# Another order of the projections in the second block of a two-block hybrid network (one NeuronCore, float32)

## The chip, the cores and the metric

The kernel runs on one core of one Trainium2 chip. The metric is the device time of one execution in microseconds (us); the time before is a median of three runs. Engine names are those of the profile: PE is TensorE (matmul), PEld its weight load, DVE is VectorE, ACT is ScalarE, POOL is GpSimd, SP is SyncE, which issues the loads of the weights.

## The reference, cut to what matters

Two blocks run one after the other on 512 positions of width 1024. The change lies in the mixer of the second. It projects the normalised input with one matrix into 14 groups of columns, lets three branches work on them, and projects the joined result with `w_out`:

```
p = xn @ w_in                       # (512, 1024) @ (1024, 3340)
mq, mk, mv, mo, mi, mf, lx, lg, aq, ak, av, iq, ik, iw = split_cols(p)
hA = mlstm_chunkwise(mq, mk, mv, mi + b_igate, mf + b_fgate)   # 4 heads of 96: matrix memory
hA = rmsnorm(hA, mlstm_norm) * sigmoid(mo)
xc = causal_depthwise_conv(lx, lru_conv_w, lru_conv_b)
hB = rglru(xc, ...) * gelu(lg)                                 # linear recurrence, 384 channels
hC = dsa_attention(aq, ak, av, iq, ik, iw)                     # 4 heads of 64, 128 chosen keys a query
mix = concatenate([hA, hB, hC]) @ w_out
x = x + rmsnorm(mix); x = x + rmsnorm(conv_ffn(rmsnorm(x)))
```

`dsa_attention` scores every admissible key for a query with `iq`, `ik` and `iw`, keeps the best 128, and runs a softmax attention with `aq`, `ak`, `av` over those alone.

## The kernel before

**Tiling.** Activations lie with the channel on the partition: eight tiles of 128 channels by 512 positions. A weight tile (128x1024, 512 KB) is loaded as `raw` by SP, rounded by ACT into `wh`, and DVE takes the remainder `wl = raw - wh`. Each step of a projection is three matmuls (activation by `wh`, activation by `wl`, remainder of the activation by `wh`). A unit of kind `f` (128 output channels by 512 positions) is 8 such steps, 24 matmuls of 512 columns. A unit of kind `tok` has the positions on the partition and 256 channels as columns; it takes two weight tiles, and is 96 matmuls of 256 columns, 24 for each of the four blocks of positions t.

**What sets the order.** Every engine works through its own list in order. The lists are written when the kernel is built, by a planner (`Model`, `Lane`, `Build`) that keeps an estimated time of each engine. `block2_mix` (L1434) walks down the table `UNITS2` (L1355): the first four entries are computed together, the others one after the other. After each step, `tick` (L200) lets every side task whose inputs are due by the estimate emit its next instructions, so that their matmuls stand between those of the projections. The engines then wait for real at whatever is not ready, and everything behind the waiting instruction on that engine's list waits too. Rounds of the top-k search are handed to DVE one by one, when it has nothing else.

**The side tasks of the mixer**, with what each waits for:
- `scores` (L1505) starts once `iq1` is done: for t = 1, 2, 3 the index scores on PE, ReLU on ACT, weighting on DVE; then 16 rounds of top-k on DVE (MAX8 and MATCH_REPLACE8 over 256, 384 or 512 columns) and the mask `mbs` of that t.
- `sparse` (L1720), sixteen steps (t, head) in three streams, needs `aq`, `ak`, `av` and the mask of its t. `sparse_out` (L1774) turns the result into `hc[6]` and `hc[7]`.
- `lrus` (L1547) needs `lx0` to `lx2`, in its last part `lg0` to `lg2`, and makes `hc[3]` to `hc[5]`.
- `memory` (L1604), four heads in two streams, needs the gates, `mk`, `mq`, and `va`, which is done with unit `t1`. Its last matmuls (128x97) are copied into two tiles `nums` (names `act<-at`, 128x194).
- `memories` (L1660), behind the last of them: maximum of the denominators (`den`), squares on ACT (128x768, twice), sums of them on DVE (`sumsq`, twice), a chain of 17 small DVE instructions ending in `rd`, and then, once unit `t2` is done and its gate `mo` went through Tanh, per half a multiplication by `rd` (128x768) and two by the gate; 12 transposes on PE, an ACT copy and a DVE subtraction for each of three tiles give `hc[0]` to `hc[2]`.

After the table, `w_out` is multiplied (`units` with `order=[3, 4, 5, 0, 1, 2, 6, 7]`, 24 matmuls of 256 columns for an output tile and half of the positions). When it comes to a tile of `hc` that is not there by the plan, it takes another that is; the first output tiles of the first half are begun with what is there.

Of the kernel before, what the change touches and what calls it, by code (L numbers as in the profile page):

```python
# [162 lines left out]
class Build:  # L163
# [1075 lines left out]
    def block1_ffn(self):  # L1239
# [114 lines left out]

    UNITS2 = [  # L1355
        ('idx',),
        ('aq0', 'f', 2312),
        ('lg0', 'f', 1928),
        ('aq1', 'f', 2440),
        ('lx0', 'f', 1544),  # L1360
        ('lx1', 'f', 1672),
        ('lx2', 'f', 1800),
        ('iq0', 'f', 3080),
        ('mk0', 'f', 384),
        ('lg1', 'f', 2056),
        ('lg2', 'f', 2184),
        ('iq1', 'f', 3208),
        ('mk1', 'f', 512),
        ('av', 'tok', 2824),
        ('mk2', 'f', 640),  # L1370
        ('mq0', 'f', 0),
        ('mq1', 'f', 128),
        ('t0', 'tok', 768),
        ('mq2', 'f', 256),
        ('t1', 'tok', 1024),
        ('ak0', 'f', 2568),
        ('ak1', 'f', 2696),
        ('t2', 'tok', 1280),
    ]

# [826 lines left out]
```

## Time and profile before

| | us |
|---|---|
| median of 3 runs (lowest, highest) | 1567.85 (1567.51, 1568.6) |
| the profiled execution: its time, its span | 1567.5, 1565.7 |
| PE busy | 1546.3 (99%) |
| DVE busy | 1101.5 (70%) |
| ACT busy | 680.5 (43%) |
| weight load (PEld) busy, beside the matmuls | 1386.4 (89%) |
| granted TensorE clock, mean | 0.999 |

The mixer of the second block takes the stretch from about 936 us to 1190 us. The rows are given below; in a timeline row the first number is the start in us from the start of the span, the second the time to the end of the last instruction of the row, and a bracket at the end is the idle time ahead of it with what ended it. Matmuls are pipelined: one that is listed with 0.28 us follows the one ahead after 0.12 us.

### The profile page before, as it was taken

What the parts mean: (1) busy time and instruction counts of PE and PEld (TensorE: products, weight loads), DVE (VectorE), ACT (ScalarE), POOL (GpSimd) and SP (SyncE); (2) the same over time, 40 slices, a digit from 0 to 9 for tenths busy, and PEclk for the clock granted to TensorE, in tenths of its full rate; (3) what the DMA queues carried; (4) which work ended last, traced back from release to release, by engine and by line L of the source; (5) the groups of instructions that cost most, each with busy time, mean ns of one, the idle gap of its engine ahead of it and who ended that gap; (6) DMA issues with size and microseconds to landing.
All of it is one profiled execution on the core that took longest, in us unless ns stands there. A gap on an engine that the chain in (4) does not pass through costs nothing.

```text
span 1565.7 us, 25299 instructions
## 1 busy us (share of the span) xinstructions
PE 1546.3 (99%) x10279; PEld 1386.4 (89%) x10281; DVE 1101.5 (70%) x2011; ACT 680.5 (43%) x1222; POOL 25.9 (2%) x89
## 2 busy tenths in 40 slices
PE   7999999999999999999999999999999999999998
PEld 6999999999999999999988877796799888888886
DVE  4899999997764576776743457899768877775224
ACT  5344544546843343443432223625565544444112
POOL 4000000000000000000000000000000000000000
PEclk9999999999999999999999999999999999999999
DMA  5322222222222333333333332231053133333221
GB/s 145 95 69 75 75 70 80 68 68 68 73 77 71 92 108 93 85 94 95 91 88 98 84 99 80 59 104 55 19 144 109 55 95 95 95 98 102 94 95 68
DMA packets 233005, 134.17 MB, mean 86 GB/s; under 512 B 6925, under 2 KB 228240, under 8 KB 232888
## 3 DMA queue, kind: packets, MB, share of 16 engines
q1 hardware_dynamic: 231448, 130.35, 28.7%
q8 instruction: 81, 1.33, 0.4%
q0 software_dynamic: 1136, 1.15, 0.3%
q10 hardware_dynamic: 304, 1.05, 0.2%
q14 instruction: 36, 0.29, 0.1%
HBM read 130.44 MB, written 2.10 MB: 85 GB/s over the span
## 4 chain that ended last, share of the span: by engine, by line
PE 97%; DVE 1%; ACT 1%; DMA 0%; issue 0%; DVEq 0%; ACTq 0%; POOLq 0%
PE mm L314 70%; PE at L314 24%; PE at L320 3%; ACT act L158 1%; DVE act L158 0%; DMA act<-in_x_dram 0%; DVE yy L158 0%; DVE wl L158 0%; ACT ys L158 0%; DVE yc L158 0%; ACT wh L158 0%; DVE nb L158 0%; DVE fx L158 0%; DVE res L158 0%; ACT e L158 0%
## 5 line engine op out<-in xcount | busy, mean ns | idle before, releaser
L314 PE MATMUL mm<-act,wh 128*128 128x256 f32 (+3 forms) x4720 | 906.2, 306 | 1.5 <-DVE act L158 0.8
L314 PEld LDWEIGHTS mm<-act,wh 128*128 128x128 f32 (+1 forms) x4720 | 692.0, 189 | 49.5 <-issue 10.9
L314 PE MATMUL mm<-act,wl 128*128 128x256 f32 (+4 forms) x2360 | 562.8, 302 | 0.0
L158 ACT ACTIVATE wh<-raw 128x1024 fp32r<-128x1024 f32 (+2 forms) x235 | 245.7, 1047 | 367.5 <-PE mm L314 187.1
L158 DVE TENSOR_TENSOR wl<-raw,wh 128x1024 fp32r<-128x1024 f32 (+2 forms) x235 | 284.5, 1211 | 168.9 <-ACT wh L158 165.9
L314 PEld LDWEIGHTS mm<-act,wl 128*128 128x128 f32 (+1 forms) x2360 | 383.1, 189 | 18.0
L158 DVE SCALAR_TENSOR_TENSOR act<-u,par,act 128x514 f32<-128x514 f32 x232 | 161.1, 748 | 2.2 <-ACT act L158 2.2
L314 PE MATMUL at<-act,wh 128*128 128x512 f32 x416 | 130.3, 394 | 0.0
L314 PEld LDWEIGHTS at<-act,wh 128*128 128x128 f32 x416 | 78.1, 188 | 18.4
L314 PE MATMUL at<-wh,act 128*128 128x512 f32 x264 | 86.0, 395 | 0.0
L314 PE MATMUL mm<-wh,act 128*128 128x256 f32 (+1 forms) x344 | 84.4, 320 | 0.0
L314 PE MATMUL at<-act,act 128*128 128x256 f32 (+9 forms) x468 | 83.5, 329 | 0.8 <-ACT act L158 0.7
L314 PE MATMUL at<-act,wl 128*128 128x512 f32 x208 | 82.0, 394 | 0.0
L158 DVE TENSOR_TENSOR act<-act,act 128x514 f32<-128x514 f32 (+4 forms) x122 | 69.7, 589 | 8.2 <-ACT act L158 7.5
L314 PEld LDWEIGHTS at<-act,act 128*128 128x128 f32 (+1 forms) x468 | 60.2, 189 | 11.1 <-issue 4.7
L158 DVE SCALAR_TENSOR_TENSOR ft<-fx,par,ft 128x512 f32<-128x512 f32 x88 | 65.8, 749 | 1.5
L158 DVE TENSOR_TENSOR fx<-mm,rB 128x514 f32<-128x514 f32 x44 | 30.5, 694 | 50.3 <-PE mm L314 50.1
L314 PEld LDWEIGHTS mm<-wh,act 128*128 128x128 f32 x344 | 57.9, 189 | 7.3 <-issue 3.4
L158 ACT ACTIVATE act<-mm 128x528 f32<-128x528 f32 (+2 forms) x64 | 35.1, 548 | 66.8 <-PE mm L314 66.7
L158 ACT ACTIVATE act<-at 128x128 f32<-128x128 f32 (+6 forms) x88 | 34.4, 413 | 67.8 <-PE at L314 50.2
L158 DVE SCALAR_TENSOR_TENSOR gy<-gx,par,gy 128x512 f32<-128x512 f32 x84 | 62.6, 748 | 1.5
L314 PEld LDWEIGHTS at<-wh,act 128*128 128x128 f32 x264 | 49.6, 188 | 11.6
(286 smaller groups left out, 1435.8 us busy)
## 6 DMA issues: line engine op xcount, KB each, us to landing
raw<-in_w_in_dram SPq DMA_DIRECT2D x82, 512.0 KB, 3.8
raw<-in_w_up_dram SPq DMA_DIRECT2D x44, 512.0 KB, 3.8
raw<-in_ffn_up_dram SPq DMA_DIRECT2D x44, 512.0 KB, 3.9
raw<-in_ffn_down_dram SPq DMA_DIRECT2D x22, 512.0 KB, 3.2
raw<-in_w_out_dram SPq DMA_DIRECT2D x20, 512.0 KB, 3.8
raw<-in_w_down_dram SPq DMA_DIRECT2D x16, 512.0 KB, 3.8
raw<-in_w_conv_out_dram SPq DMA_DIRECT2D x8, 512.0 KB, 3.8
raw<-in_w_down_dram SPq DMA_DIRECT2D x8, 384.0 KB, 3.3
```

The source lines that it names most:

```text
L158: return f(*a, **k)
L314: self.nc.tensor.matmul(out, lhsT, rhs, start=start, stop=stop)
L320: self.nc.tensor.transpose(out, src, self.ident[p0 : p0 + k, p0 : p0 + k])
```

## The change

The entries of `UNITS2` get another order; nothing else is edited. Entries and their number stay the same, and so do the instructions of each engine; what the planner puts between the projections follows the new order.

```
     UNITS2 = [
         ('idx',),
+        ('iq0', 'f', 3080),
+        ('iq1', 'f', 3208),
         ('aq0', 'f', 2312),
-        ('lg0', 'f', 1928),
-        ('aq1', 'f', 2440),
         ('lx0', 'f', 1544),
         ('lx1', 'f', 1672),
         ('lx2', 'f', 1800),
-        ('iq0', 'f', 3080),
+        ('lg0', 'f', 1928),
         ('mk0', 'f', 384),
+        ('aq1', 'f', 2440),
+        ('mk1', 'f', 512),
         ('lg1', 'f', 2056),
+        ('mk2', 'f', 640),
         ('lg2', 'f', 2184),
-        ('iq1', 'f', 3208),
-        ('mk1', 'f', 512),
         ('av', 'tok', 2824),
-        ('mk2', 'f', 640),
         ('mq0', 'f', 0),
+        ('ak0', 'f', 2568),
         ('mq1', 'f', 128),
         ('t0', 'tok', 768),
+        ('ak1', 'f', 2696),
         ('mq2', 'f', 256),
         ('t1', 'tok', 1024),
-        ('ak0', 'f', 2568),
-        ('ak1', 'f', 2696),
         ('t2', 'tok', 1280),
     ]
```

On PE, the list is the same up to the start of the mixer's units and again from the second output tile of `w_out` on; some 800 entries between are rearranged. Before, this stood on PE from the last product of the memory (`128x97`) to the first transposes of its result (`ident` with a name of 128x768); `mm_11435` and `mm_11436` are unit `t2`, `mm_11889` is `w_out`, the `128x64` and those with `e` or `mbs` are the sparse attention:

```order
L314 MATMUL at_11684<-act_10935,act_11505 128x97
L314 MATMUL mm_11435<-wh_11342,act_9580 128x256
...
L320 MATMUL at_11748<-ident,e_11740 128x128 x3
...
L314 MATMUL at_11829<-act_11334,act_10107 128x384
...
L314 MATMUL mm_11436<-wh_11342,act_9857 128x256
L320 MATMUL at_11879<-ident,e_11865 128x128 x3
L314 MATMUL mm_11889<-act_10700,wh_11442 128x256 x2
...
L314 MATMUL at_11936<-act_11334,act_10107 128x512
...
L314 MATMUL at_11944<-act_10631,act_10762 128x64 x4
L320 MATMUL at_11954<-ident,act_11898 128x128 x2
```

Now the same stretch reads (`mm_11562` is unit `t2`, `mm_11953` is `w_out`, `act_12007` and `act_12011` the two halves of the memory's result):

```order
L314 MATMUL at_11917<-act_11037,act_11837 128x97
L314 MATMUL mm_11562<-wh_11565,act_9765 128x256
...
L314 MATMUL mm_11562<-wh_11565,act_9857 128x256
L314 MATMUL mm_11953<-act_10742,wh_11582 128x256 x2
...
L314 MATMUL mm_11953<-act_10816,wh_11582 128x256 x2
L314 MATMUL mm_11953<-act_10816,wl_11583 128x256
L320 MATMUL at_12015<-ident,act_12007 128x128 x2
L320 MATMUL at_12015<-ident,act_12011 128x128 x2
L320 MATMUL at_12023<-ident,act_12007 128x128 x2
L320 MATMUL at_12023<-ident,act_12011 128x128 x2
L314 MATMUL mm_11953<-act_12020,wh_11582 128x256 x2
```

What moved: between the last product and the first transposes there were 95 matmuls, 45 of `t2` and `w_out` and 50 of the sparse attention with its transposes; there are 15 now, 6 of `t2` and 9 of `w_out`. The sparse attention stands ahead of the memory's last head.

On ACT, in the same place, the list had the squares (`128x768`) ahead of the Tanh of the gates (`128x512`, `128x1024`), with copies and exponentials of the sparse attention between:

```order
L158 ACTIVATE act_11237<-at_11684 128x2x97
L158 ACTIVATE act_10762<-at_11748 128x384
...
L158 ACTIVATE act_11779<-act_11236 128x768
L158 ACTIVATE e_11789,sll_11769<-at_11756,snb_11768 128x384
L158 ACTIVATE act_11575<-mm_11435,R 128x256
L158 ACTIVATE act_11797<-act_11237 128x768
...
L158 ACTIVATE act_11575<-mm_11436,R 128x256
L158 ACTIVATE act_10477<-act_10477 128x512
L158 ACTIVATE act_11575<-act_11575 128x1024
```

Now, from the copy of the memory's last products on:

```order
L158 ACTIVATE act_11569<-at_11917 128x2x97
L158 ACTIVATE act_11653<-mm_11562,R 128x256
L158 ACTIVATE act_10694<-act_10694 128x512
L158 ACTIVATE act_11653<-act_11653 128x1024
L158 ACTIVATE wh_11960<-raw_11563 128x1024
L158 ACTIVATE act_11970<-act_11568 128x768
L158 ACTIVATE wh_11978<-raw_11580 128x1024
L158 ACTIVATE act_11983<-act_11569 128x768
```

What moved: the Tanh of the gates and two weight roundings of `w_out` now stand ahead of the squares.

On DVE, the part of `memories` from `den` to the small chain had narrow instructions of the sparse attention between its own; now it has two remainders `wl` of 128x1024:

```order
L158 SCALAR_TENSOR_TENSOR den<-act_11236 128x8
L158 TENSOR_REDUCE sumsq<-act_11779 128x8
L158 SCALAR_TENSOR_TENSOR den<-act_11237 128x8
L158 TENSOR_SCALAR act_10763<-at_11781,srl_11724 128x64
L158 TENSOR_SCALAR act_10763<-at_11785,srl_11728 128x64
L158 TENSOR_REDUCE sumsq<-act_11797 128x8
L158 TENSOR_TENSOR den<-den,em 128x16
```

Now, from the first `den` on:

```order
L158 SCALAR_TENSOR_TENSOR den<-act_11568 128x8
L158 TENSOR_TENSOR wl_11961<-raw_11563,wh_11960 128x1024
L158 TENSOR_REDUCE sumsq<-act_11970 128x8
L158 SCALAR_TENSOR_TENSOR den<-act_11569 128x8
L158 TENSOR_TENSOR wl_11979<-raw_11580,wh_11978 128x1024
L158 TENSOR_REDUCE sumsq<-act_11983 128x8
L158 TENSOR_TENSOR den<-den,em 128x16
```

What moved: the remainders wait for the roundings of ACT that stand ahead of the squares there.

## Rows read from the trace of the kernel before

**Rows 1.** The page: busy time and share of PE, and the shares of the engines in the chain of work that ended last.

```profile
PE 1546.3 (99%) x10279; PEld 1386.4 (89%) x10281; DVE 1101.5 (70%) x2011; ACT 680.5 (43%) x1222; POOL 25.9 (2%) x89
...
PE 97%; DVE 1%; ACT 1%; DMA 0%; issue 0%; DVEq 0%; ACTq 0%; POOLq 0%
```

**Rows 2.** Busy time of each engine by stretch (from and to in us, length, then us busy with the number of instructions for PE, PEld, DVE, ACT and POOL, the granted clock, the DMA share and GB/s).

```profile
1000.00:1057.00 57.00, 57.00 (x370) 49.51 (x366) 54.61 (x124) 22.20 (x46) 0.22 (x2) 1.00 0.30 84
...
1120.00:1143.00 23.00, 21.99 (x158) 18.41 (x159) 15.61 (x39) 12.99 (x26) 0.20 (x2) 1.00 0.16 47
1143.00:1190.00 47.00, 46.52 (x395) 46.51 (x395) 35.09 (x73) 33.32 (x67) 0.10 (x1) 1.00 0.47 133
```

**Rows 3.** Timeline of PE at the end of the mixer: the last products of the memory (the row joins 128x64 and 128x97), the last matmuls of unit `t2`, two steps of `w_out`, the two waits of that stretch, the first transposes of the memory's result.

```profile
1110.81 1.48 PE L314 MATMUL at<-act,act 128*128 128x64 f32 x12
...
1124.27 0.28 PE L314 MATMUL mm<-wh,act 128*128 128x256 f32 x1
...
1125.87 0.40 PE L314 MATMUL mm<-act,wh 128*128 128x256 f32 x2
1126.10 0.28 PE L314 MATMUL mm<-act,wl 128*128 128x256 f32 x1
1126.96 0.88 PE L314 MATMUL at<-act,act 128*128 128x64 f32 x6 [0.58 <-ACT act L158]
...
1129.50 1.89 PE L314 MATMUL at<-act,act 128*128 128x64 f32 x16 [0.16 <-ACT act L158]
1131.23 0.61 PE L320 MATMUL at<-ident,act 128*128 128x128 f32 x4
```

**Rows 4.** Timeline of ACT there: the copies of the memory's last products, a square, the copy and the two Tanh of the gates, two weight operations, the copy of the first transposed tile.

```profile
1112.32 0.56 ACT L158 ACTIVATE act<-at 128x194 f32<-128x194 f32 x2 [1.07 <-PE at L314]
...
1114.20 0.85 ACT L158 ACTIVATE act<-act 128x768 f32<-128x768 f32 x1
...
1124.59 0.47 ACT L158 ACTIVATE act<-mm,R 128x256 f32<-128x256 f32 x1 [0.97 <-PE mm L314]
1124.96 1.57 ACT L158 ACTIVATE act<-act 128x512 f32<-128x512 f32 x2
...
1127.46 1.06 ACT L158 ACTIVATE wh<-raw 128x1024 fp32r<-128x1024 f32 x1
1128.41 1.09 ACT L158 ACTIVATE act<-at 128x512 f32<-128x512 f32 x2
...
1131.88 0.69 ACT L158 ACTIVATE act<-at,wn 128x512 fp32r<-128x512 f32 x1 [1.43 <-PE at L320]
```

**Rows 5.** Timeline of DVE there: the sum of a square, the first and the last of the small chain, the multiplication by `rd` and the two by the gate (second half), a weight remainder, the subtraction for the first tile.

```profile
1115.38 0.95 DVE L158 TENSOR_REDUCE sumsq<-act 128x8 f32<-128x768 f32 x1
...
1118.09 0.17 DVE L158 TENSOR_TENSOR den<-den,em 128x16 f32<-128x16 f32 x1
...
1121.51 0.17 DVE L158 TENSOR_TENSOR rd<-rd,rsy 128x16 f32<-128x16 f32 x1
...
1127.25 0.94 DVE L158 TENSOR_TENSOR act<-act,rd 128x768 f32<-128x768 f32 x1
1128.22 1.03 DVE L158 SCALAR_TENSOR_TENSOR act<-act,act 128x256 f32<-128x256 f32 x2
...
1129.49 1.21 DVE L158 TENSOR_TENSOR wl<-raw,wh 128x1024 fp32r<-128x1024 f32 x1
...
1132.77 0.74 DVE L158 SCALAR_TENSOR_TENSOR act<-at,wn,act 128x512 fp32r<-128x512 f32 x1
```

**Rows 6.** Busy time by stretch, as rows 2, at the end of the span.

```profile
1560.00:1566.00 6.00, 0.00 (x0) 0.00 (x0) 2.59 (x8) 0.20 (x1) 0.00 (x0) 0.78 0.34 130
```

**Rows 7.** Timeline of PE at the end of the span: its last two rows.

```profile
1558.30 0.40 PE L314 MATMUL mm<-wl,act 128*128 128x512 f32 x1
1558.53 0.39 PE L314 MATMUL mm<-wh,act 128*128 128x512 f32 x1
```

**Rows 8.** Timeline of PE at the start of the span: transposes (`ident`) and a projection in 128x264.

```profile
14.83 2.72 PE L320 MATMUL at<-ident,act 128*128 128x128 f32 x9 [2.65 <-DVE act L158]
...
18.96 1.08 PE L314 MATMUL mm<-act,wh 128*128 128x264 f32 x4
19.84 0.64 PE L314 MATMUL mm<-act,wl 128*128 128x264 f32 x2
20.28 1.62 PE L320 MATMUL at<-ident,act 128*128 128x128 f32 x10
21.94 0.51 PE L314 MATMUL mm<-act,wh 128*128 128x264 f32 x2
...
27.42 0.65 PE L314 MATMUL mm<-act,wh 128*128 128x264 f32 x4
27.91 0.42 PE L314 MATMUL mm<-act,wl 128*128 128x264 f32 x2
```

**Rows 9.** Timeline of DVE: the last round of top-k for t = 3 and its mask.

```profile
1106.32 0.68 DVE L158 MAX8 m<-sc 128x8 f32<-128x512 f32 x1
...
1107.11 0.67 DVE L158 MATCH_REPLACE8 sc<-m,sc 128x512 f32<-128x512 f32 x1
...
1107.82 0.43 DVE L158 TENSOR_SCALAR mbs<-sc 128x512 bf16<-128x512 f32 x1
```

**Rows 10.** Timeline of ACT: the table load ahead of the recurrence's square roots.

```profile
999.13 1.28 ACT L158 ACT_TABLE_LOAD   x1
```

More of the change, by code (lines that the diff above doesn't have):

```diff
@@ L1356 @@
         ('idx',),
+        ('iq0', 'f', 3080),
+        ('iq1', 'f', 3208),
         ('aq0', 'f', 2312),
-        ('lg0', 'f', 1928),
-        ('aq1', 'f', 2440),
         ('lx0', 'f', 1544),
@@ L1362 @@
         ('lx2', 'f', 1800),
-        ('iq0', 'f', 3080),
+        ('lg0', 'f', 1928),
         ('mk0', 'f', 384),
+        ('aq1', 'f', 2440),
+        ('mk1', 'f', 512),
         ('lg1', 'f', 2056),
+        ('mk2', 'f', 640),
         ('lg2', 'f', 2184),
-        ('iq1', 'f', 3208),
-        ('mk1', 'f', 512),
         ('av', 'tok', 2824),
-        ('mk2', 'f', 640),
         ('mq0', 'f', 0),
+        ('ak0', 'f', 2568),
         ('mq1', 'f', 128),
         ('t0', 'tok', 768),
+        ('ak1', 'f', 2696),
         ('mq2', 'f', 256),
         ('t1', 'tok', 1024),
-        ('ak0', 'f', 2568),
-        ('ak1', 'f', 2696),
         ('t2', 'tok', 1280),
```

## The prediction

> **What bounds the kernel now.** First the page: PE is busy for 99% of the span, and the chain that ended last is PE for 97% of its length [rows 1]. Such a kernel gets shorter only where PE waits, and longer by each microsecond that a new order makes PE wait. The change adds and removes no instruction on any engine, so the question is where PE waits before and where it will. The table by stretch says how much there is to win [rows 2]: in the rearranged part PE is full in 1000:1057 and leaves 1.01 us of 1120:1143 and 0.48 us of 1143:1190. The timeline names the larger waits, 0.58 and 0.16 us for sparse attention [rows 3]. DVE, 54.61 of 57 us in 1000:1057, is nearly as full there, with its top-k rounds; in 1120:1143 it has room (15.61 of 23), and ACT too.
>
> So the best that any order of these units can do is to take away about 1.5 us, half of what a measurement of this kernel tells from no change (0.2%, 3.1 us). Nearly all that can happen is a new wait.
>
> **The change part by part.** I laid each engine's new list against the durations and looked for places where a list comes to an instruction whose input is late. Three matter.
>
> *The end of the mixer: +14.9.* Let T be the end of the last product of the memory. Before, that is 1110.81 + 1.48 = 1112.29, and the first transposes of the normalised result start at 1131.23 [rows 3]: 18.9 us in which PE worked through sparse attention and unit t2, with about a microsecond of waits. The work of ACT and DVE from the copies to the gated result was covered. Now the list has 15 projection matmuls there. Their step is (1126.10 - 1125.87) / 2 = 0.12 us [rows 3], so PE has 1.8 us to do and then stands at the transposes. What it waits for, from T, with the durations of rows 4 and 5:
>
> ACT: copies, 0.6. The copy of the last block of t2 waits for PE's six matmuls and starts at 0.9; 0.37 later (1124.59 to 1124.96) the two Tanh, 1.57, to 2.75. A rounding wh, 0.95 (1127.46 to 1128.41), to 3.7; first square 0.85, to 4.55; second wh, to 5.5; second square, to 6.35.
>
> DVE: den is short; the remainder wl has to wait for the wh at 3.7 and takes 1.2, to 4.9; sumsq 0.95, to 5.8; second wl 1.2, to 7.0; second sumsq, to 7.9. The small chain takes 1121.68 - 1118.09 = 3.6, to 11.5. Scaling and gating one half takes 0.97 + 1.03 = 2.0, so the first half stands at 13.5, the second at 15.4.
>
> PE again: four transposes, of which two can go at 13.5, then ACT's copy 0.69 and DVE's subtraction 0.74 [rows 3 to 5]: 15.4 + 0.4 + 0.7 + 0.75 = 17.25, when hc[0] is there. The transposes of hc[2] stand behind the three matmuls with it, and need a PSUM tile that this same subtraction frees: 17.25 + 0.35 + 0.6 = 18.2, and with copy and subtraction 19.7. From there on PE has all its inputs. In those 19.7 us it works 1.8 us, 12 transposes of about 0.11 us each, 1.3, and six matmuls on hc[0] and hc[1], 0.7: 3.8. It waits 15.9, against 1.0 before: +14.9. Neither engine has other work in the way, since the sparse attention is finished; and nobody's work covers it, as w_out's next output tiles stand behind hc[2] on PE's list. The bounds: if the scaling of the halves ran as tightly as their overlap allows, or the squares slipped between the Tanh, 2 us less; with an added semaphore hop of some 0.1 us at each of a dozen handovers, 1.5 us more.
>
> *A weight tile of av: +1.2.* In the new order the recurrence's last units (lx0 to lx2) lie just ahead of lg0 and the memory keys, and the second weight tile of av comes soon after. On ACT its wh stands behind the table load (1.28) [rows 10] and three square roots; on DVE its wl (1.21) [rows 5] stands behind the recurrence's scans and three rounds of top-k. Adding these lists up, wl is there 1.2 us after PE wants it. If the rounds were one fewer it costs nothing; if a wait that I missed precedes it, about another 1.2. The trace of before has no such wait, so 0 to 2.5.
>
> *The masks: 0.* The scores start earlier, as iq0 and iq1 come first, and DVE works on the rounds from then on. But sparse attention comes earlier too: on PE three scores of t = 3 stand together ahead of the last memory head. A round is 0.68 + 0.67 us and the mask 0.43 [rows 9]; adding DVE's list, mask 3 is done within a microsecond of where PE comes to it. With DVE as full as in 1000:1057 a miss of a few rounds is possible: four are 5.6 us. I take 0, and keep 0 to 6. What waits behind it on PE would be all else, but the memory's ACT and DVE work would catch up meanwhile, so not all of it would add up.
>
> The moved loads on SP keep the order of the units. In 1000:1057 and 1120:1143 PE waits for no transfer and the DMA share stands below a third, near half in 1143:1190 [rows 2]: nothing.
>
> *The clock: +3.* In the new tail PE stands from T + 1.8 to T + 13.5, 11.7 us, with nothing between. What such a pause does is seen once in this trace, at its end: the last matmul ends at 1558.9 [rows 7], and in 1560:1566 the mean granted clock is 0.78 [rows 6], which is full clock (2.4 GHz) until some 4.4 us after that end and the lower level, 1.2 GHz, from there. So the pause should bring the lower level. What it costs is read at the start: four matmuls of 128x264 take 0.88 us at 18.96 and 0.49 at 27.42, nearly double, and the ten transposes from 20.28 lie between both levels: PE had worked without a break from 14.83 when its steps became short [rows 8]. In the tail the slow transposes and matmuls lengthen the chain by about 0.8; of the work behind T + 19.7 some 3 to 6 us run at half speed, less what the work since T + 15.4 has already brought, and lose half of that: 2.2. Together 3.0, with 1.5 to 4 as bounds.
>
> The Trainium skill (TensorE: Matmul & The Clock Gate, section Why this matters for your kernels) says that idle gaps between bursts of matmuls put the clock back to half rate. The trace agrees as far as it goes, with the one fall of rows 6; no run here shows a gap of this length inside a stage. By that rule the sum keeps the 3.0, and without it the forecast would be the first rival below.
>
> **Sum.** 1567.5 (the profiled execution, 1.8 us above its span) + 14.9 + 1.2 + 0 + 3.0 = 1586.6. The median of the runs shown is 0.35 us above that execution, so 1587.
>
> **The rivals.** *The clock stays up* (14 in 100). The fall after the last matmul came at the end of the program, where every engine winds down; if a pause inside a stage is judged otherwise, the same tail gives 1567.85 + 14.9 + 1.2 = 1584. Only the fall at the end speaks against it.
>
> *Late masks as well* (10 in 100). DVE is the bound, not the list of PE: mask 3 comes four rounds late at the three scores. Price 5.6, with the rest of the sum 1592. It needs DVE to be later than its added durations by what four rounds take; before, DVE had waits of its own between rounds, which are the reason for it.
>
> *Not slower: the tail is covered* (8 in 100). The mechanism is the one that covers it before: if the memory's last products were ready so late in PE's list that sparse attention still stood behind them, or ACT and DVE had done the squares and the gates of the earlier halves before T, the chain behind T would be short. The order decides it: it pays out if at least 16 us of PE work stand between the last product and the first transposes, and there are 1.8. Then all that remains is the 1.0 to 1.5 us of waits of before that the new order may remove: 1566.5 to 1568, the same by what can be told. To be faster by over 3.1 us the change would have to free PE of waits that rows 2 do not have; only an effect outside the rearranged stretch could, as from the weight loads of later stages, and I see none.
>
> That the change does nothing is excluded by the lists, where some 800 entries of PE differ.
>
> **How the numbers follow.** Forecast 68 in 100, clock stays 14, late masks 10, covered or without effect 8, of which 2 in 100 are faster by over 0.2% and 6 within it. Slower by over 0.2%: 0.92. Low end: the tail at 13, no wait for av, the clock at its lower bound, 1582, or without the fall of the clock 1581; I put it at 1580. High end: the forecast with the hops, with 2.5 for av and part of the masks, 1593.
>
> **What would show it.** After the last 128x97 product of the memory the timeline of PE has a handful of matmuls, then a wait of 11 to 12 us that ends with DVE at a transpose, one of about 2 us, and two of 1 to 1.5 us at matmuls or transposes of w_out. The table by stretch shows some 16 us of PE idle in one piece of 25 us, a granted clock below 1.00 there, and matmuls of 128x256 at 0.23 us each just behind. DVE shows the remainder wl ahead of each sumsq. In the part that is av's first blocks, a wait of about a microsecond for DVE. I am wrong if PE has no wait above 3 us in the mixer, if the clock reads 1.00 all through it, or if a wait on a mask (scores of 128x512) is the largest.

## The result: 1.2% slower, and the profile after

| | before | after |
|---|---|---|
| median (lowest to highest), us | 1568.22 (1567.51 to 1569.81) | 1587.35 (1586.54 to 1588.1) |
| span of the profiled execution, us | 1565.7 | 1586.2 |
| PE busy, us | 1546.3 | 1553.5 |

The ratio is 1.0121 (95% interval 1.0105 to 1.0137): 19.1 us more, where 1587 us was forecast. The page of the changed kernel, to set beside [rows 1]:

```profile
PE 1553.5 (98%) x10279; PEld 1392.1 (88%) x10281; DVE 1100.5 (69%) x2011; ACT 680.1 (43%) x1222; POOL 25.7 (2%) x89
...
PE 96%; DVE 2%; ACT 1%; issue 0%; DMA 0%; DVEq 0%; ACTq 0%; POOLq 0%
```

The instructions are the same, and still PE is busy 7 us longer: that is the mark of a slower clock (a step of `w_out` takes 0.21 us at 1160, where the granted clock reads 0.50, and 0.12 us from 1162 on, at 1.00). The table by stretch of the changed kernel (columns as in [rows 2]) says where the time went:

```profile
1000.00:1057.00 57.00, 56.14 (x345) 49.06 (x344) 53.54 (x121) 25.29 (x46) 0.22 (x2) 1.00 0.27 75
1057.00:1084.00 27.00, 27.00 (x175) 21.65 (x175) 24.15 (x62) 10.64 (x35) 0.00 (x0) 1.00 0.20 58
1084.00:1100.00 16.00, 16.00 (x74) 10.59 (x73) 13.42 (x26) 7.77 (x19) 0.00 (x0) 0.89 0.24 67
1100.00:1120.00 20.00, 19.59 (x122) 14.71 (x123) 5.69 (x14) 8.06 (x22) 0.10 (x1) 1.00 0.00 1
1120.00:1143.00 23.00, 19.06 (x136) 16.55 (x134) 7.81 (x17) 12.74 (x29) 0.10 (x1) 0.96 0.00 1
1143.00:1170.00 27.00, 17.61 (x102) 15.80 (x103) 15.16 (x35) 7.49 (x14) 0.00 (x0) 0.66 0.22 60
```

PE is full up to 1084, but for 0.86 us, and idle for 13.3 us between 1120 and 1170; over the last 27 of these the granted clock is 0.66 in the mean. PE's timeline there, from the last products of the memory on:

```profile
1136.24 1.03 PE L314 MATMUL at<-act,act 128*128 128x97 f32 x8
...
1138.78 0.28 PE L314 MATMUL mm<-act,wl 128*128 128x256 f32 x1
1150.12 0.69 PE L320 MATMUL at<-ident,act 128*128 128x128 f32 x2 [11.06 <-DVE act L158]
1152.05 1.54 PE L320 MATMUL at<-ident,act 128*128 128x128 f32 x6 [1.24 <-DVE act L158]
...
1157.51 0.58 PE L314 MATMUL mm<-act,wh 128*128 128x256 f32 x1 [0.20 <-DVE act L158]
...
1163.84 0.51 PE L314 MATMUL mm<-act,wh 128*128 128x256 f32 x2 [0.48 <-ACT act L158]
```

The one wait of 11.06 us is the largest piece of the loss: the transposes wait for DVE. The timeline of DVE in it:

```profile
1140.95 1.23 DVE L158 TENSOR_TENSOR wl<-raw,wh 128x1024 fp32r<-128x1024 f32 x1 [3.10 <-ACT wh L158]
1142.09 0.95 DVE L158 TENSOR_REDUCE sumsq<-act 128x8 f32<-128x768 f32 x1
1142.96 0.16 DVE L158 SCALAR_TENSOR_TENSOR den<-act 128x8 f32<-128x8 f32 x1
1143.04 1.22 DVE L158 TENSOR_TENSOR wl<-raw,wh 128x1024 fp32r<-128x1024 f32 x1
1144.17 0.94 DVE L158 TENSOR_REDUCE sumsq<-act 128x8 f32<-128x768 f32 x1
...
1148.44 0.17 DVE L158 TENSOR_TENSOR rd<-rd,rsy 128x16 f32<-128x16 f32 x1
1148.65 0.96 DVE L158 TENSOR_TENSOR act<-act,rd 128x768 f32<-128x768 f32 x1
...
1151.57 1.02 DVE L158 SCALAR_TENSOR_TENSOR act<-act,act 128x256 f32<-128x256 f32 x2
```

DVE is not overloaded here; it is the chain that is long, one small instruction after another, with two weight remainders in it, and with nothing of PE's beside it. Each step against the forecast, from T = 1136.24 + 1.03 = 1137.27:

| step | forecast T + | measured T + |
|---|---|---|
| second sumsq done | 7.9 | 7.8 |
| small chain done (rd) | 11.5 | 11.3 |
| first transposes | 13.5 | 12.9 |
| second half scaled and gated | 15.4 | 15.3 |
| w_out on hc[2] | 20.5 (19.7 and 0.8 for the clock) | 20.2 |

The first transposes came earlier than forecast: they need only the first 128 columns of the half, and of the two gate instructions the first delivers these.

### The profile page after: what moved, and what is told of

Its sections match the earlier page's. It is cut to its first block, busy times and chain, and to the rows that moved or that the text cites. A ratio compares the mean times of both kernels' runs of the same rounds, so it can differ in the third digit from the quotient of the medians.

```text
span 1586.2 us, 25305 instructions
## 1 busy us (share of the span) xinstructions
PE 1553.5 (98%) x10279; PEld 1392.1 (88%) x10281; DVE 1100.5 (69%) x2011; ACT 680.1 (43%) x1222; POOL 25.7 (2%) x89
## 3 DMA queue, kind: packets, MB, share of 16 engines
q0 software_dynamic: 1136, 1.15, 0.3%
## 4 chain that ended last, share of the span: by engine, by line
PE 96%; DVE 2%; ACT 1%; issue 0%; DMA 0%; DVEq 0%; ACTq 0%; POOLq 0%
PE mm L314 69%; PE at L314 24%; PE at L320 3%; DVE act L158 1%; ACT act L158 1%; DMA act<-in_x_dram 0%; DVE wl L158 0%; DVE yy L158 0%; DVE sumsq L158 0%; DVE rsa L158 0%; ACT ys L158 0%; DVE yc L158 0%; DVE res L158 0%; DVE rsy L158 0%; ACT wh L158 0%
## 5 line engine op out<-in xcount | busy, mean ns | idle before, releaser
L314 PE MATMUL mm<-wh,act 128*128 128x256 f32 (+1 forms) x344 | 90.4, 328 | 0.9 <-DVE act L158 0.9
L320 PE MATMUL at<-ident,act 128*128 128x128 f32 (+6 forms) x298 | 47.5, 279 | 14.9 <-DVE act L158 14.9
```

Of the source, the lines that this page charges most:

```text
L314: self.nc.tensor.matmul(out, lhsT, rhs, start=start, stop=stop)
L320: self.nc.tensor.transpose(out, src, self.ident[p0 : p0 + k, p0 : p0 + k])
```

## The experiments

Two explanations were set against each other. The tail: with the attention keys early, the sparse attention is over before the memory's last head, and nothing covers the normalisation. The front: the early index queries put top-k rounds between recurrence and projections and cost the time there. The first four runs take the change apart by its table.

**Attention keys back** (in the changed table):

```
-        ('ak0', 'f', 2568),          # behind mq0
...
-        ('ak1', 'f', 2696),          # behind t0
...
         ('t1', 'tok', 1024),
+        ('ak0', 'f', 2568),
+        ('ak1', 'f', 2696),
         ('t2', 'tok', 1280),
```

> The changed table with only the attention keys ak0 and ak1 put back between t1 and t2. Tail theory (the attention keys' early place moves the sparse attention ahead of the memory's last head and leaves its normalisation uncovered): some 21 us of PE work stand again between the last memory product and the first transposes of its result, no wait above 1 us there, the clock at 1.00 in the mixer, 1567 to 1570 us. Rival, the front (the early index queries put top-k rounds between recurrence and projections, and that costs the time): nothing of the front has changed, so 1582 us or more.

1571.15 us, 1.0023 of the kernel before (1.0013 to 1.0032). The clock is 1.00 in the mixer, its largest wait 1.04 us. So 16 of the 19 us go with the keys' place. The 3.1 that stay are more than expected; 2.7 of them are waits (4.1 us in the mixer against 1.4 before), the largest two at `w_out` for a tile of `hc` (1.04 us at 1138.73) and at av (0.90 us at 1009.78).

**Attention keys forward** (in the old table):

```
         ('mq0', 'f', 0),
+        ('ak0', 'f', 2568),
         ('mq1', 'f', 128),
         ('t0', 'tok', 768),
+        ('ak1', 'f', 2696),
         ('mq2', 'f', 256),
         ('t1', 'tok', 1024),
-        ('ak0', 'f', 2568),
-        ('ak1', 'f', 2696),
```

> The old table with only ak0 and ak1 moved forward, to the places that they have in the new one (behind mq0 and behind t0); the index queries stay late. Tail theory: about 2 us of PE work between the last memory product and the transposes, a wait of 10 to 12 us in one piece there, the clock down to the lower level, 1584 to 1590 us. Front rival: 1567 to 1570 us, since the front is the old one.

1591.07 us, 1.015 (1.0133 to 1.0167): slower than the whole change, and above the range expected; the long wait is shorter than expected. PE's waits in the mixer (what is waited for, us in all, times, longest):

```profile
PE at L320 <- DVE act L158: 9.5, 2, 8.3
PE at L314 <- ACT e L158: 3.3, 1, 3.3
```

The tail is there, with 8.3 us in its first wait, and a wait of 3.35 us stands ahead of a score of the sparse attention:

```profile
1123.98 1.84 PE L314 MATMUL at<-act,act 64*128 64x512 f32 x2 [3.35 <-ACT e L158]
```

The mask is not what it waits for. With the index queries late, the mask of t = 3 is ready at 1110.9 (DVE, `mbs`) and not at 1096.1 as in the changed kernel, but its first matmul on PE comes at 1117.3. The wait ends with an exponential on ACT, and on ACT's list that stands behind eight exponentials of the memory, which start only at 1119.45, after 8.85 us in which ACT was idle. The rest of the change (the early queries and the entries that moved with them) is thus worth some 4 us once the keys are early; which of these entries it is was not tried, and together they still lose.

**Index queries forward** (in the old table):

```
         ('idx',),
+        ('iq0', 'f', 3080),
+        ('iq1', 'f', 3208),
         ('aq0', 'f', 2312),
...
-        ('iq0', 'f', 3080),
...
-        ('iq1', 'f', 3208),
```

> The old table with only iq0 and iq1 moved to the second and third place. Tail theory: some 19 us of PE work cover the chain, as before or better: 1566.5 to 1569 us. Front rival: most of the loss is there, 1580 us or more.

1570.48 us, 1.0016 (1.0007 to 1.0026). The long chain is covered, as expected, but the run is 2.4 us slower than before, not equal. Its waits in the mixer:

```profile
PE mm L314 <- DVE act L158: 1.4, 2, 1.0
PE mm L314 <- ACT act L158: 0.5, 1, 0.5
PE at L314 <- ACT act L158: 0.3, 1, 0.3
PE at L314 <- DVE act L158: 0.3, 1, 0.3
```

That is 2.5 us, against the 1.4 of the kernel before; the other 1.3 us are in the busy time of PE and were not traced to an instruction. The waits do not stand in the front: the two largest, 0.97 us at 1136.42 and 0.41 at 1140.85, are `w_out` waiting for a tile of `hc`.

**One key back** (in the changed table, ak1 alone between t1 and t2):

```
-        ('ak1', 'f', 2696),          # behind t0
...
         ('t1', 'tok', 1024),
+        ('ak1', 'f', 2696),
```

> The changed table with only ak1 put back between t1 and t2, ak0 forward. About 9.5 us of PE work stand between the last memory product and the transposes in place of 1.8. Tail theory: the wait shrinks by as much, to some 8 us in several pieces; 1575 to 1580 us, at the lower end if the clock stays up. Front rival: no change against the changed kernel, 1587 us.

1578.43 us, 1.0068 (1.0053 to 1.0083). The loss is about halved with half of the cover, as the tail theory has it, and the front is out as the main cause. But the wait is another one than expected: the transposes of the memory's result wait for nothing now, and the largest waits, 3.1 and 1.6 us, are for exponentials of the sparse attention. PE's wait, which is ahead of transposes of these exponentials (`e`):

```profile
1138.42 1.97 PE L320 MATMUL at<-ident,e 128*128 128x128 f32 x8 [3.13 <-ACT e L158]
```

ACT had waited there for a reduction of the sparse attention on DVE (`snb`, started at 1136.87), and on DVE's list that stands behind the memory's small chain (`rd` ended at 1134.82) and its first scaled half. The long chain costs here through what stands behind it on DVE. The waits of the mixer come to 6.7 us, 5.3 more than before; the other half of the loss is slow work: PE is busy 5.6 us longer than before, and behind this wait the granted clock is 0.50 from 1138 to 1146.

The next runs are on the parts of the tail: the clock and the chain.

**The first wait filled** (in the changed kernel, ahead of the transposes for hc[0]; the output of these matmuls is overwritten):

```
+    if c == 0:
+        for _ in range(42):
+            nc.tensor.matmul(pt[:, :SEQ], hc[3][:, 0, 0:P], hc[3][:, 0, :SEQ], start=True, stop=True)
```

> The changed kernel with 42 matmuls of 128x512 (a tile of hc[3] by itself, into the PSUM tile that the first transposes overwrite) on PE's list right ahead of the first transposes of the memory's result: 42 x 0.23 = 9.7 us of work for nothing in a wait of 11.1 us. ACT and DVE are untouched. If the fall of the clock costs 2 to 3 us of the 19, as the prediction has it: the granted clock reads 1.00 through the tail, the matmuls of w_out behind it take 0.12 us at once, and the time is 1584 to 1586 us, below the changed kernel although it does more. If the clock costs nothing and the chain on ACT and DVE is all: 1587 to 1588 us.

1587.48 us, no gain: by the expectation that would mean that the clock costs nothing, but the table by stretch shows that it still fell:

```profile
1145.00:1150.00 5.00, 3.07 (x14) 2.06 (x12) 4.52 (x17) 0.00 (x0) 0.00 (x0) 1.00 0.32 93
1150.00:1155.00 5.00, 3.33 (x16) 2.71 (x16) 3.02 (x5) 1.51 (x3) 0.00 (x0) 0.77 0.00 0
1155.00:1160.00 5.00, 4.66 (x22) 4.07 (x22) 0.75 (x1) 0.47 (x1) 0.00 (x0) 0.55 0.00 0
```

The clock stayed up through the filled wait (1.00 to 1152) and fell behind it, in the stop and go of the transposes (waits of 1.53 and 1.49 us ahead of them). From the first matmul of w_out to its third output tile it takes 25.4 us (1136.86 to 1162.29), hardly less than without the filling (26.0 in the profile above, 25.5 in the one further down). The run didn't do what it was made for.

**The same with transposes** (88 of the identity in place of the 42 matmuls):

> As the run before, but with 88 transposes of the 128x128 identity in place of the 42 matmuls (88 x 0.11 = 9.7 us). If transposes hold the clock as matmuls do: the same 1584 to 1586 us. If they do not count: the clock falls in the tail as in the changed kernel, the transposes themselves get slower and run past the end of the chain (up to 5 us), and the time is 1588 to 1593 us.

1586.76 us, no clear gain either. The clock reads 1.00 in 1141:1145 and 1145:1150 here too, the 88 take 9.77 us, and the tail is 25.6 us: transposes held the clock like the matmuls did, and it fell at the same place.

**The whole tail filled** (`fill(tile, n)` stands for n matmuls into that tile; shortened):

```
+    if c == 0: fill(pt[:, :SEQ], 47)
+    if c == 1: fill(pt[:, :SEQ], 4)
     for t in range(4):
+        if c == 0 and t == 2: fill(pt[:, 256:512], 13)
         tr(...)
+    if c == 2: fill(another PSUM tile, 4)
```

> The changed kernel with PE kept at work through the whole tail, not only through its first wait: 47 matmuls of 128x512 ahead of the first transposes, 13 of 128x256 between the first and the second half, 4 and 4 of 128x512 around the later transposes, all for nothing, some 14 us in waits of 13 us and more. If the lower clock costs what the prediction has (3.0, or 2.4 by the rows behind the tail): the granted clock reads 1.00 through the whole mixer, the stretch from the first matmul of w_out to its third output tile is 23.5 to 24 us in place of 26.0, and the time 2 to 3 us below the changed kernel run beside it. If the clock costs nothing: no difference.

The changed kernel ran beside it:

> The changed kernel itself, beside the run with the filled tail on the same chip: 1586.5 to 1588 us, a wait of 11 us ahead of the transposes, the lower clock from some microseconds into it to the 1161st microsecond.

1585.29 us (1584.36 to 1585.61) against 1586.73 (1585.95 to 1587.45): 1.4 us less, where 2 to 3 were expected. In the tail the clock is now 1.00:

```profile
1145.00:1150.00 5.00, 4.89 (x22) 3.73 (x20) 4.38 (x20) 0.00 (x0) 0.00 (x0) 1.00 0.46 133
1150.00:1155.00 5.00, 4.62 (x33) 4.07 (x33) 3.71 (x7) 1.38 (x2) 0.00 (x0) 1.00 0.00 0
1155.00:1160.00 5.00, 4.83 (x37) 4.45 (x36) 1.29 (x2) 0.69 (x1) 0.00 (x0) 1.00 0.02 3
```

The memory's last product, the first matmul of w_out, its first on hc[2] and the third output tile, in the filled run:

```profile
1136.39 1.03 PE L314 MATMUL at<-act,act 128*128 128x97 f32 x8
...
1137.99 0.40 PE L314 MATMUL mm<-act,wh 128*128 128x256 f32 x2
...
1156.74 0.39 PE L314 MATMUL mm<-act,wh 128*128 128x256 f32 x1 [0.17 <-DVE act L158]
...
1161.30 0.51 PE L314 MATMUL mm<-act,wh 128*128 128x256 f32 x2 [0.47 <-ACT act L158]
```

and the first and the last of them in the changed kernel beside it:

```profile
1136.45 0.39 PE L314 MATMUL mm<-act,wh 128*128 128x256 f32 x2
...
1161.92 0.51 PE L314 MATMUL mm<-act,wh 128*128 128x256 f32 x2 [0.48 <-ACT act L158]
```

From the first matmul of w_out to its third output tile: 1161.30 - 1137.99 = 23.3 us, against 1161.92 - 1136.45 = 25.5. That is what the clock costs in the tail: 2.2 us, got back by giving PE work for nothing (2.7 against the first profile of the changed kernel, where the stretch is 26.0). Of it 1.4 show in the medians; the profiled execution of the filled kernel has a short fall of the clock in 1084:1100 (0.89) that the other has not.

**Squares first** (in the changed kernel; shortened):

```
     for q in range(2):
         stt(den ...)
         S.activation(sqs[q], nums[q][:, :, :, 0:96], AF.Square)
-        yield self.due(sq)
-        V.tensor_reduce(v2(ss), sq, axis=AX.X, op=ADD)
+    for q in range(2):
+        yield self.due(sqs[q])
+        V.tensor_reduce(v2(ss, q), sqs[q], axis=AX.X, op=ADD)
```

> The changed kernel with both squares of the memory's normalisation issued before either sum, so that the second rounding wh and the second remainder wl of w_out no longer stand between the two sums on ACT and DVE. Tail theory: the chain loses one wl of 1.2 us; the long wait is 9.9 us in place of 11.1, and the time 1585.5 to 1586.5 us. If the long wait is for something else than this chain (the gates of t2, a transfer), it stays at 11.1 and the time at 1587.

1585.71 us, in the range expected, though by the time alone it can't be told from the changed kernel (1585.95 to 1587.45 in the run just named). The long wait shrank as expected, by the one remainder wl:

```profile
1147.42 0.69 PE L320 MATMUL at<-ident,act 128*128 128x128 f32 x2 [9.85 <-DVE act L158]
```

No version was found that is faster than the kernel before: the mixer there has 1.4 us of PE's waits in all, which is less than one of these comparisons can tell.

## Why the prediction was right

**The bound** was read rightly: at 99% busy on PE, no order could win much, and a new wait was all that could happen.

**The end of the mixer, +14.9: right in mechanism and in size.** Filled with work, so at full clock, the stretch from w_out's first matmul to its third output tile is 23.3 us. PE's own part of it is 48 matmuls of 0.12, 12 transposes of 0.11 and the wait of 0.47 ahead of the third tile: 5.6 + 1.3 + 0.5 = 7.4. The other 15.9 us are the uncovered chain, which is the forecast number; less the 1.0 us of waits before, 14.9. That it agrees to a tenth is chance: counted from T, as in the forecast, w_out comes to hc[2] at T + 19.3 in the filled run (T is 1136.39 + 1.03 = 1137.42 there, and the matmul starts at 1156.74), where 19.7 stood. Runs with the keys back, with one key back and with the keys forward alone move the loss with the cover, and the run with the squares first moves the long wait with the chain. Of the signs, the long wait came as forecast (11.06 us); the three behind it were 1.24, 0.20 and 0.20 us, where one of 2 and two of 1 to 1.5 were named, and PE's waits in the tail add up to 12.7 us and not to 16. The forecast counted them at full clock; at the lower clock PE's own transposes and matmuls take up part of that time (PE's busy time is 7 us longer).

**The weight tile of av, +1.2: the size was near (0.86), the reason was not, so this is luck.** I had PE wait for wl on DVE. The wait is there, one block of positions later:

```profile
1009.82 0.39 PE L314 MATMUL mm<-wh,act 128*128 128x256 f32 x1 [0.86 <-DVE act L158]
```

DVE's list at this place:

```profile
1006.12 1.20 DVE L158 TENSOR_TENSOR wl<-raw,wh 128x1024 fp32r<-128x1024 f32 x1
1007.24 0.68 DVE L158 TENSOR_TENSOR act<-act,act 128x512 f32<-128x512 f32 x1
1007.95 1.22 DVE L158 TENSOR_TENSOR_SCAN act<-act 128x512 f32<-128x512 f32 x1
1009.10 0.67 DVE L158 TENSOR_TENSOR act<-mm,rB 128x512 f32<-128x512 f32 x1
```

The wl ended at 1007.32 and PE's matmul on it started at 1007.37: hardly late. What PE waited for at 1009.82 is the end of the instruction at 1009.10 (1009.77), which reads a PSUM tile of `mm`, by its place that of the unit ahead (lg2), and so frees it for av's second block. It stood behind the scans of the recurrence on the same list. That a matmul's own output tile must be free was missing in my list of what it needs.

**The masks, 0: right, with more room than I thought.** Mask 3 was ready at 1096.1, and its first matmul on PE came at 1100.4:

```profile
1100.38 0.39 PE L314 MATMUL at<-mbs,identb 128*128 128x512 bf16 x1
```

That is 4.3 us, where I had within one. Part of it is a slower PE: in the second profile, without the fall of the clock ahead of this place, it is 2.6 us (1096.4 to 1099.0). Two waits of 0.25 and 0.16 us behind it come to 0.4.

**The clock, +3.0: right in mechanism, 2.2 to 2.7 in the tail.** The clock by stretch in the tail of the changed kernel:

```profile
1139.00:1141.00 2.00, 0.06 (x1) 0.00 (x0) 0.05 (x1) 2.00 (x4) 0.00 (x0) 1.00 0.00 0
1141.00:1143.00 2.00, 0.00 (x0) 0.00 (x0) 2.00 (x3) 2.00 (x3) 0.00 (x0) 0.51 0.00 0
...
1159.00:1161.00 2.00, 2.00 (x11) 2.00 (x11) 0.00 (x0) 0.00 (x0) 0.00 (x0) 0.50 0.00 0
1161.00:1163.00 2.00, 2.00 (x17) 2.00 (x16) 0.00 (x0) 0.00 (x0) 0.00 (x0) 0.87 0.00 0
```

PE's last matmul ended at 1139.06, and from 1141 on the granted clock is the lower level, until about 1161.4. Of the two terms of the 3.0 the lengthening of the chain was right (0.8; w_out comes to hc[2] at T + 20.2 in both profiles of the changed kernel and at T + 19.3 in the filled run), and the slow work behind hc[2] was put too high: 2.2, where from hc[2] to the third tile the two profiles have 6.3 and 5.8 us and the filled run 4.6, that is 1.2 to 1.8. The forecast took the price of the lower clock from slow steps at the start of the span [rows 8], and that reading is not borne out. The granted clock of the kernel before reads 1.00 there:

```profile
10.00:20.00 10.00, 7.35 (x29) 5.89 (x30) 7.87 (x22) 8.16 (x15) 9.00 (x16) 1.00 0.78 197
```

So what makes those steps slow is not shown. The tail itself shows the price: a step of 0.21 us at a granted clock of 0.50 and of 0.12 at 1.00. The page of the Trainium skill named in the prediction (TensorE: Matmul & The Clock Gate, section Why this matters for your kernels) says that idle gaps between bursts put the clock back; here the trace shows it inside a stage, and the rival by which the clock stays up is out. Its section Part 4: PE-mode transpose holds that transposes do not count for the clock as other matmuls do; the run with 88 transposes (1.00 through the filled wait, as with matmuls) does not agree, as far as these are the transposes meant there: the profile lists them as MATMUL.

**The sum.** Without the short fall of the clock ahead of the tail, which the profile beside the filled run has not: 14.9 for the chain, 1.3 for the small waits (0.86, 0.25, 0.16), 2.2 for the clock, 18.4. That execution reaches the third tile of w_out at 1161.92, the kernel before at 1143.50 (both with the wait of 0.48 ahead of it):

```profile
1143.50 0.50 PE L314 MATMUL mm<-act,wh 128*128 128x256 f32 x2 [0.48 <-ACT act L158]
```

That is 18.4. The first profile of the changed kernel had the short fall too, and a span 1.9 us longer. That the median comes within 0.4 us of the forecast is therefore partly luck: the clock's part in the tail was put too high, and in some executions a fall that the forecast did not have made up for it.

**What the prediction did not have** is a cost of the early index queries other than by the masks. Moved alone they cost 2.4 us, and with the keys back the rest of the change costs 3.1. The sum above closes without it; whether the tail hides it in the whole change was not tried.

**Open:** the 1.3 us of PE's busy time in the run with the queries forward, and the cause of the short fall of the clock.

## What to carry to other kernels

On an engine that is full, an order of work is judged by what covers the long chains of the other engines, not by how early their inputs are ready: here the same sparse attention was done earlier and was missed later, as the work that had stood beside the memory's normalisation. List, for each long chain on ACT and DVE, the work of PE that stands behind its start and ahead of its first use; where that is shorter than the chain, the difference is a first estimate of the loss. Here it held to about half a microsecond for the chain with nothing beside it; with half of the cover the loss came by another way, through the work that stood behind the chain on DVE's list, and the lower clock came on top in both. To the inputs of each instruction add the tile that it writes: who has to empty it, and what stands ahead of that on its list.

## What was not expected of the hardware

The clock fell in three more ways. In 1084:1100 of the changed kernel it went to 0.50 for about 3 us while PE was fully busy (rows of two microseconds):

```profile
1088.00:1090.00 2.00, 2.00 (x10) 1.11 (x9) 2.00 (x4) 2.00 (x5) 0.00 (x0) 0.96 0.00 0
1090.00:1092.00 2.00, 2.00 (x5) 0.97 (x5) 2.00 (x3) 2.00 (x6) 0.00 (x0) 0.50 0.11 27
1092.00:1094.00 2.00, 2.00 (x10) 1.46 (x10) 1.97 (x5) 2.00 (x7) 0.00 (x0) 0.68 1.01 284
```

PE worked there through the memory's float32 products of 128x512, the spreads of 4x512 ahead of them and projections between; the cause is not shown. The second profile of the very same kernel has 1.00 in that stretch, so it comes and goes between executions, at 1.4 us or so a time (an estimate: half of about 3 us); its four times beside the filled tail lie in two pairs, about 1586.0 and 1587.4 us. And with the long wait filled it fell without any wait above 1.6 us, in the stop and go behind it: filling the largest hole alone brought nothing that could be measured. With one key back it fell inside a single wait of 3.1 us: the granted clock reads 1.00 in 1134:1136, 0.65 in 1136:1138 and 0.50 in the four stretches of two microseconds behind.
